# Fetching the second blocks of late operands earlier in a transformer-layer kernel on one core

## The chip, the cores and the metric

The kernel runs on one NeuronCore of a Trainium2 chip. The metric is the device time of one execution in microseconds (us). A program has five instruction queues that matter here: PE (TensorE, the matmuls), DVE (VectorE), ACT (ScalarE), POOL (GpSimd) and SP (SyncE, which here only issues DMAs). Each queue runs its instructions in the order in which they were written down, and waits at an instruction until what it depends on is done.

## The reference

The kernel computes one layer of a decoder trunk on 512 tokens (T) with a model width of 2048, a feed-forward width of 5632 and a per-layer embedding of 256. Cut to what matters:

```
h   = rmsnorm(x)
u, v_sgu, q, k, v, g_a, g_b = split(h @ w_in)
y_a = u * spatial_gating(rmsnorm(v_sgu))
y_b = stick_breaking_attention(rmsnorm(q), rmsnorm(k), v)
x  += (sigmoid(g_a) * (y_a @ w_up_a) + sigmoid(g_b) * (y_b @ w_up_b)) @ w_o
x  += (silu(gate) * up) @ w_ffn_out       # gate, up = split(rmsnorm(x) @ w_ffn_in)
x  += sigmoid(rmsnorm(x) @ w_ple_gate) * (p @ w_ple)
```

## The kernel before

**Arithmetic.** Every product is made of float32 numbers cut into a high and a low part, and so of three matmuls per product: high times high, low times high, high times low. A product of a 256-wide block of operand with weights is done either *plain* (8 products of quarter blocks) or in a *Strassen-like* form with 7 products ("S"), whose operands are sums and differences of the quarters. The weights of an S unit are summed on DVE (L373), split on ACT (high, L357) and DVE (low, L354). The operands are likewise split on ACT (L284) and DVE (L285), both called by the helper `split_into`.

**Stages, in order of time.** The combined input projection with attention and gating (0 to about 830 us); the two up projections, whose merged result is eight blocks called `mix` (to 996 us); `w_o`, which multiplies the eight `mix` blocks, giving eight output blocks j = 0 to 7 called `x1` (from 996.2 us); the small `w_ple` products; `w_ffn_in` (about 1175 to 2040 us), whose outputs are 22 blocks called `hid`; `w_ffn_out` in three passes, over 8, 8 and 6 of the `hid` blocks (starting at about 2041, 2202 and 2362 us); and the gate (about 2485 to 2661 us). `mix`, `x1`, `hid` and `x2` are stored to DRAM when they are made (SP at L1332, L1376, L1398, L1434) and fetched again as operands of the next stage.

**Late operands.** Such a fetched operand is a `Form` of kind "S" (`late_form`). It comes in two parts. The *first block* is a load of 1024 columns (512 KB) by `Form.fetch`. When the operand has its turn, a *step* splits the four quarters (ACT L284 and DVE L285, 128x1024 each) and the operand can be used plain; `HALF` says that in a stage the first four operands are used plain for the first output block (j = 0), the last four for the first two (j = 0 and 1). At that step the operand is put on a list, `seconds`. Its *second block* is the same 1024 columns again, loaded into a piece of 1280 by `Form.fetch_second`; DVE makes sums from it (L525) and three or four more tiles are split, after which the operand serves as an S operand. What is done with it depends on whether the operand's plain use is over (`form.used`) when the second block arrives: if so, a two-tile-wide sum and one split of four tiles (4x256) follow; if not, three single sums and a split of three tiles (3x256) follow at once, and a split of one tile (256) when the plain use ends.

**What sets the order.** The order of all queues is fixed when the program is built. `tick` is called once per unit of matmuls. It looks at the next three operands (`AHEAD`) of the list `builds`, fetches at most one first block, takes at most one step of the first operand in the list, and may fetch one second block. All raw blocks live in one arena, `wholes`, of 13312 columns; `fits` tries whether the pieces asked for, and 1024 more, find room there, and everything that is taken from it waits for the last user of that place. All loads and stores at the lines above stand in SP's one queue, together with the loads of the weights (L337, L339, L341).

Each operand's second load and its splits are written by the generator `plain_first`, its waiting condition by `second_arrived`. The results of `w_o` for doubled outputs (from j = 2) leave the matmul banks through `Pair.rest` (L787), and are added to the residual by `onto` (L792).

Of the kernel before, what the change touches and what calls it, by code (L numbers as in the profile page):

```python
# [39 lines left out]
AHEAD, WAIT = 3, 2  # L40
# [28 lines left out]
def hybrid_layer(  # L69
# [84 lines left out]
    parts, wholes = Arena("parts", PARTS, F32R), Arena("wholes", WHOLES, F32)  # L154
# [8 lines left out]
    def fits(sizes):  # L163

        before = parts.holes, wholes.holes
        parts.holes, wholes.holes = list(parts.holes), list(wholes.holes)
        try:
            for arena, n, how in sizes + [(wholes, 1024, "low")]:
                arena.take(n, how)
            return True  # L170
        except ValueError:
            return False
        finally:
            parts.holes, wholes.holes = before
# [15 lines left out]
    builds, seconds, stages = deque(), deque(), iter(range(1 << 30))  # L190
# [13 lines left out]
    def traced():  # L204
        return nc.cur_bb.bb.instructions

    def tick():

        clock[0] += 1
        last, units = traced()[-1], dict(newest)  # L210
        urgent = [f for f in seconds if f.used]
        sizes = []
        for f in list(builds)[: 0 if urgent else AHEAD]:
            sizes += [s for s in f.sizes if s[0] is parts]
            raw = [(wholes, 1024, "old")]
            if not f.there and f.ready() and (fits(sizes + raw) or fits(raw * 3)):
                f.fetch()
                break
        if builds and builds[0].ready() and builds[0].arrived() and fits(builds[0].sizes):
            builds.popleft().step()  # L220
        elif seconds and fits([(wholes, 5 * 256, "old")]):
            f = (urgent or seconds)[0]
            if f.used or not any(b.stage == f.stage and b.ready() and not b.there
                                 for b in list(builds)[:AHEAD]):
                f.fetch_second()
        while waiting and waiting[0][0] <= clock[0]:
            heapq.heappop(waiting)[2]()
        for i in reversed(traced()):
            if i is last:
                break  # L230
            if i.engine in units:
                tc.add_manual_dep(
                    i, units[i.engine],
                    mybir.DependencyInfo(mybir.DependencyClass.NoSync,
                                         mybir.DependencyReason.DATA),
                    reason="in its place among the units")
# [389 lines left out]
    class Pair:  # L626
# [21 lines left out]
        def add(self, kind, ws, xs, prepare=True):  # L648
# [6 lines left out]
            if kind == "P":  # L655
                for u, ((wh, wl), (xh, xl)) in enumerate(zip(ws, xs)):
                    for ps, bs in zip(self.ends(), ((3, 2), (1, 0))):
                        for k, b in enumerate(bs):
                            first = start and u + k == 0

                            mark(mm3(ps, wh[:, b], wl[:, b], xh[k], xl[k],
                                     first and not self.both, stop and u == n - 1 and k == 1,
                                     first and self.both and b < 2))
                    if prepare and u == 0:
                        prepare_late()
                    tick()
                return
# [5 lines left out]
            for i, ((name, h), (w, x)) in enumerate(zip(HALVES, PRODUCTS)):  # L673
                for u, ((wh, wl), t) in enumerate(zip(ws, xs)):
                    first, last = start and u == 0, stop and u == n - 1
                    if i < self.doubled:
                        ps = self.at(i)
                        both = ps, wh[:, w], t[:, x].rearrange("p s c -> p (s c)")
                        low = ps[:, :256], wl[:, w], t[:, x, 0]

                        work = (low, both) if u else (both, low)
                        for k, (out, l, r) in enumerate(work):
                            m = nc.tensor.matmul(out, l, r, start=first and k == 0,  # L683
                                                 stop=last and k == 1)
                        mark(m)
                    else:


                        ps = self.at(name)[:, 256 * h : 256 * h + 256]
                        ends = not (self.both and name in "yz") and (h == 1 or name == "z")  # L690
                        mark(mm3(ps, wh[:, w], wl[:, w], t[:, x, 0], t[:, x, 1],
                                 first and h == 0, last and ends))
                if stop:
                    next(mix)
                if i == 2:
                    prepare_late()
                if i in TICKS[n]:
                    tick()
# [161 lines left out]
    def ple_pair(j, weights=None):  # L860
        slot, ((wh, wl),) = weights.get() if weights else next_weights()
        if not weights:
            prepare_early()
            prepare_late()
        o = wide()
        banks = bank(), bank()
        for k in range(2):
            xh, xl = (x.own(k * T, (k + 1) * T) for x in ps_p)
            for i, ps in enumerate(banks):
                s = 2 * i + k  # L870
                mm3(ps, wh[:, s], wl[:, s], xh, xl, k == 0, k == 1)
        for i, ps in enumerate(banks):
            nc.scalar.activation(o[:, i * T : (i + 1) * T], ps, AF.Copy)
        d = tc.dram_tile([P, 1024], F32, name=nm("ple"))
        nc.sync.dma_start(out=d, in_=o)
        ple_spill[j] = d
        slots.append(slot)
        tick()
# [537 lines left out]
    for c, units in enumerate(hs):  # L1416
        first, at = at, at + len(units)
# [137 lines left out]
```

## Time and profile before

| what | us |
|---|---|
| three runs | 2667.51, 2673.16, 2673.37 |
| median of the three | 2673.16 |
| the profiled execution's own time | 2668.2 |
| its span (first to last instruction) | 2666.5 |
| PE matmul busy | 2640.4 |
| DVE busy | 2236.4 |
| ACT busy | 1413.9 |

The span is what the trace covers; the execution's own time has 1.7 us more around it. In the views, a row names the line, the engine, the operation, the tile written and the tiles read with shapes, then times in us. "idle before <- X" says how long the engine stood still ahead of that instruction and what it was waiting for. A name such as `ps` is a matmul bank, `parts` the arena of split operands, `wholes` that of raw blocks, `whi` and `wlo` the high and low parts of weights.

### The profile page before, as it was taken

To read this page: it belongs to the slowest core of one execution; us is meant where nothing else is said; L and a number is where in the kernel's file an instruction comes from. 1 tells how busy PE (TensorE), PEld (TensorE's weight loads), DVE (VectorE), ACT (ScalarE), POOL (GpSimd) and SP (SyncE) were. 2 spreads that over 40 slices of the span, in tenths; PEclk is the share of its full clock that TensorE was granted. 3 is DMA by queue.
4 is the path that set the end of the run, shared out by engine and by line. 5 is a ranking of instruction groups with operands and counts; after the bars stand their busy time and mean duration, and the time that the engine had idled before them with its cause. 6 is when DMAs were issued, how large, how long until landed. Compare 5 with 4: busy or idle time off the path is not lost.

```text
span 2666.5 us, 42598 instructions
## 1 busy us (share of the span) xinstructions
PE 2640.4 (99%) x15354; PEld 2312.4 (87%) x15354; DVE 2236.4 (84%) x3791; ACT 1413.9 (53%) x2245; POOL 453.4 (17%) x557
## 2 busy tenths in 40 slices
PE   8999999999999999999999999999999999999999
PEld 7888898888998888888888888888888888889898
DVE  8687878787887658989889888888889989989876
ACT  7656565655554334576444444444445445455643
POOL 0222322222220001101111111111110211211010
PEclk9999999999999999999999999999999999999999
DMA  7577777677775669988888878888787989988884
GB/s 227 158 190 174 185 173 187 171 182 197 179 188 186 214 212 264 239 265 223 220 218 207 210 194 207 203 203 202 197 209 223 263 220 277 226 248 246 252 229 134
DMA packets 293875, 560.16 MB, mean 210 GB/s; under 512 B 26400, under 2 KB 140832, under 8 KB 293664
## 3 DMA queue, kind: packets, MB, share of 16 engines
q1 hardware_dynamic: 231408, 442.08, 50.4%
q0 software_dynamic: 62256, 115.37, 27.0%
q8 instruction: 120, 1.97, 0.3%
q14 instruction: 91, 0.75, 0.1%
HBM read 505.97 MB, written 51.38 MB: 209 GB/s over the span
## 4 chain that ended last, share of the span: by engine, by line
PE 88%; DVE 5%; ACT 2%; DMA 2%; issue 1%; POOL 0%; SPq 0%; POOLq 0%; DVEq 0%; ACTq 0%
PE ps L683 49%; PE ps L295 10%; PE ps L296 10%; PE ps L294 10%; PE small L683 6%; DVE wlo L354 2%; DVE out L742 1%; PE small L1145 1%; PE small L1021 1%; DMA wholes<-x 1%; DMA wholes<-w_in 1%; ACT whi L357 1%; DVE wholes L373 0%; PE small L1095 0%; DVE parts L285 0%
## 5 line engine op out<-in xcount | busy, mean ns | idle before, releaser
L683 PE MATMUL ps<-parts,whi 128*128 128x512 f32 x4200 | 1404.7, 398 | 3.7 <-DVE out L787 3.1
L357 ACT ACTIVATE whi<-wholes 128x512 fp32r<-128x512 f32 (+3 forms) x941 | 872.5, 940 | 727.6 <-DVE wholes L373 270.5
L354 DVE TENSOR_TENSOR wlo<-wholes,whi 128x512 fp32r<-128x512 f32 (+3 forms) x941 | 982.7, 1079 | 65.8 <-ACT whi L357 64.0
L683 PEld LDWEIGHTS ps<-parts,wlo 128*128 128x128 f32 x4200 | 788.9, 188 | 178.4 <-DVE wlo L354 1.1
L683 PE MATMUL ps<-parts,wlo 128*128 128x256 f32 x4200 | 832.0, 279 | 0.0
L683 PEld LDWEIGHTS ps<-parts,whi 128*128 128x128 f32 x4200 | 676.4, 189 | 10.2 <-issue 4.5
L294 PE MATMUL ps<-parts,whi 128*128 128x256 f32 (+1 forms) x1822 | 598.9, 330 | 8.0 <-ACT parts L284 5.6
L295 PE MATMUL ps<-parts,whi 128*128 128x256 f32 (+1 forms) x1838 | 605.9, 330 | 0.8 <-DVE parts L285 0.8
L296 PE MATMUL ps<-parts,wlo 128*128 128x256 f32 (+1 forms) x1838 | 605.8, 330 | 0.0
L295 PEld LDWEIGHTS ps<-parts,whi 128*128 128x128 f32 x1838 | 348.4, 190 | 39.0 <-DVE parts L285 2.4
L294 PEld LDWEIGHTS ps<-parts,whi 128*128 128x128 f32 x1822 | 344.6, 190 | 41.5 <-ACT parts L284 6.7
L296 PEld LDWEIGHTS ps<-parts,wlo 128*128 128x128 f32 x1838 | 348.8, 190 | 30.8
L373 DVE TENSOR_TENSOR wholes<-wholes 128x256 f32<-128x256 f32 x822 | 345.1, 420 | 21.7 <-DMA wholes<-w_ffn_in 2.6
L742 DVE TENSOR_TENSOR out<-out,ps 128x256 f32<-128x256 f32 x490 | 202.9, 416 | 149.9 <-ACT out L739 149.4
L361 POOL DMA_DIRECT2D wholes<-w_ffn_in x170 | 148.0, 870 | 691.2 <-DVE wholes L373 197.4
L361 POOL DMA_DIRECT2D wholes<-w_in x132 | 116.3, 882 | 523.1 <-DMA wholes<-w_in 146.8
L683 PE MATMUL small<-parts,whi 128*128 128x512 f32 x480 | 190.3, 396 | 0.0
L285 DVE TENSOR_TENSOR parts<-wholes,parts 128x1024 fp32r<-128x1024 f32 (+3 forms) x148 | 138.1, 945 | 23.0 <-ACT parts L284 23.0
L284 ACT ACTIVATE parts<-wholes 128x1024 fp32r<-128x1024 f32 (+3 forms) x148 | 119.3, 830 | 55.1 <-DVE wholes L525 33.3
L739 ACT ACTIVATE out<-ps 128x256 f32<-128x256 f32 x258 | 95.7, 382 | 49.9 <-PE ps L683 46.4
L361 POOL DMA_DIRECT2D wholes<-w_ffn_out x64 | 55.6, 869 | 358.3 <-DMA wholes<-w_ffn_out 136.5
L1395 ACT ACTIVATE out<-out 128x512 f32<-128x512 f32 x44 | 27.9, 634 | 159.2 <-DVE out L1394 159.2
(123 smaller groups left out, 1750.2 us busy)
## 6 DMA issues: line engine op xcount, KB each, us to landing
wholes<-w_ffn_in SPq DMA_DIRECT2D x170, 384.0 KB, 5.6
wholes<-w_in SPq DMA_DIRECT2D x132, 384.0 KB, 5.0
wholes<-w_ffn_in SPq DMA_DIRECT2D x170, 256.0 KB, 4.8
wholes<-w_ffn_in POOLq DMA_DIRECT2D x170, 256.0 KB, 5.4
wholes<-w_in SPq DMA_DIRECT2D x132, 256.0 KB, 4.0
wholes<-w_in POOLq DMA_DIRECT2D x132, 256.0 KB, 5.0
wholes<-w_ffn_out SPq DMA_DIRECT2D x64, 384.0 KB, 6.3
wholes<-x SPq DMA_DIRECT2D x45, 512.0 KB, 5.6
```

Source lines behind the costliest of these rows:

```text
L284: return (nc.scalar.activation(hi, src, AF.Copy), nc.vector.tensor_tensor(out=lo, in0=src, in1=hi.bitcast(F32), op=ALU.subtract))
L285: nc.vector.tensor_tensor(out=lo, in0=src, in1=hi.bitcast(F32), op=ALU.subtract))
L294: nc.tensor.matmul(ps, sh, mh, start=start, stop=False)
L295: nc.tensor.matmul(ps, sh, ml, start=False, stop=False)
L296: return nc.tensor.matmul(ps, sl, mh, start=False, stop=stop)
L354: in_turn(nc.vector.tensor_tensor(out=self.lo[:, blocks], in0=r, in1=h.bitcast(F32), op=ALU.subtract))
L357: in_turn(nc.scalar.activation(h, r, AF.Copy))
L361: nc.gpsimd.dma_start(out=raw[:, 3:5], in_=self.src[:, 1:3], accum_op=ALU.add)
L373: in_turn(nc.vector.tensor_tensor(out=o, in0=x, in1=y, op=ALU.add))
L683: m = nc.tensor.matmul(out, l, r, start=first and k == 0, stop=last and k == 1)
L739: in_turn(nc.scalar.activation(out, x, AF.Copy, scale=scale))
L742: in_turn(nc.vector.tensor_tensor(out=out, in0=x, in1=y, op=op))
```

## The change

In `tick`, three things change. The fetch of a second block no longer is the alternative to an operand's step (`elif`), but may stand in the same tick. It is no longer refused while one of the next three operands of the stage has a first block that is ready and not yet fetched; instead, room must be there for the second block and for the first blocks of all of those. And the test of room comes last.

```
         if builds and builds[0].ready() and builds[0].arrived() and fits(builds[0].sizes):
             builds.popleft().step()
-        elif seconds and fits([(wholes, 5 * 256, "old")]):
+        if seconds:
             f = (urgent or seconds)[0]
-            if f.used or not any(b.stage == f.stage and b.ready() and not b.there
-                                 for b in list(builds)[:AHEAD]):
+            first = [] if f.used else [b for b in list(builds)[:AHEAD]
+                                       if b.stage == f.stage and b.ready() and not b.there]
+            if fits([(wholes, 5 * 256, "old")] + [(wholes, 1024, "old") for _ in first]):
                 f.fetch_second()
```

The changed program has one line more, so that a line from L228 on has a number higher by one (L516 is L517 there). PE, POOL and SP have as many instructions as before; DVE has 12 more and ACT 6 more, because six operands' second blocks now arrive before their plain use is over.

**Place 1: SP around the start of `w_o`.** `mix_773_8245` is the seventh of the eight `mix` blocks, `mix_774_8246` the eighth, `mix_770_8242` the fourth. SP before, from the load of the seventh operand's first block on:

```order
L516 DMA wholes_74<-mix_773_8245 128x1024
L339 DMA wholes_74<-w_o 128x2x256
L341 DMA wholes_74<-w_o 128x768
L1332 DMA mix_774_8246<-wholes_74 128x1024
L337 DMA wholes_74<-w_o 128x1024
L516 DMA wholes_74<-mix_774_8246 128x1024
L337 DMA wholes_74<-w_o 128x1024
L516 DMA wholes_74<-mix_770_8242 128x1024
L516 DMA wholes_74<-xT 128x1024
```

SP of the change, from the last load of `xT` ahead of the same store on:

```order
L517 DMA wholes_74<-xT 128x1024
L340 DMA wholes_74<-w_o 128x2x256
L342 DMA wholes_74<-w_o 128x768
L1333 DMA mix_774_8246<-wholes_74 128x1024
L338 DMA wholes_74<-w_o 128x1024
L517 DMA wholes_74<-mix_773_8245 128x1024
L517 DMA wholes_74<-mix_774_8246 128x1024
L338 DMA wholes_74<-w_o 128x1024
L517 DMA wholes_74<-mix_771_8243 128x1024
L517 DMA wholes_74<-mix_773_8245 128x1024
```

The seventh operand's first block moved from two weight loads ahead of the store of the eighth block to behind it, next to the eighth operand's first block; its place in the arena overlaps what that store reads, so that it waits for the store to land. ACT and DVE split the eighth operand first and then the seventh. The fourth operand's second block is not in the rows of the change because it went far ahead, to directly behind that operand's first block.

**Place 2: DVE ahead of the first doubled output of `w_o` (j = 2).** L787 (L788 in the change) takes the results out of the banks that j = 2 is to reuse. DVE before:

```order
L525 TENSOR_TENSOR wholes_74<-wholes_74 128x256
L285 TENSOR_TENSOR parts_73<-wholes_74,parts_73 128x256
L525 TENSOR_TENSOR wholes_74<-wholes_74 128x256
L285 TENSOR_TENSOR parts_73<-wholes_74,parts_73 128x256
L354 TENSOR_TENSOR wlo0_77<-wholes_74,whi0_76 128x1280
L354 TENSOR_TENSOR wlo0_77<-wholes_74,whi0_76 128x512
L285 TENSOR_TENSOR parts_73<-wholes_74,parts_73 128x3x256
L787 TENSOR_TENSOR out_1049_9527<-ps_1044_9512,out_1049_9527 128x512
L787 TENSOR_TENSOR out_1049_9527<-ps_1043_9505,out_1049_9527 128x512
```

DVE of the change, up to the same two rows and the two behind them:

```order
L286 TENSOR_TENSOR parts_73<-wholes_74,parts_73 128x256
L374 TENSOR_TENSOR wholes_74<-wholes_74 128x256
L286 TENSOR_TENSOR parts_73<-wholes_74,parts_73 128x256
L374 TENSOR_TENSOR wholes_74<-wholes_74 128x256
L788 TENSOR_TENSOR out_1042_9541<-ps_1037_9521,out_1042_9541 128x512
L788 TENSOR_TENSOR out_1042_9541<-ps_1036_9514,out_1042_9541 128x512
L793 TENSOR_TENSOR wholes_74<-wholes_74,out_1042_9541 128x1024
L355 TENSOR_TENSOR wlo0_77<-wholes_74,whi0_76 128x1280
L355 TENSOR_TENSOR wlo0_77<-wholes_74,whi0_76 128x512
```

The low split of a weight slot (two rows) and a split of three operand tiles stood directly ahead of L787; in the change that weight split stands behind, and the sums and the three-tile splits of the late second blocks are some ten rows further ahead.

**Place 3: SP around the start of the first pass of `w_ffn_out`.** In the program of before `hid_1200` is the first operand of the pass, `hid_1206` the seventh, `hid_1207` the eighth; in the change the same blocks are `hid_1199`, `hid_1205` and `hid_1206`. SP before:

```order
L516 DMA wholes_74<-hid_1206_10919 128x1024
L516 DMA wholes_74<-hid_1207_10920 128x1024
L339 DMA wholes_74<-w_ffn_out 128x2x256
L341 DMA wholes_74<-w_ffn_out 128x768
L337 DMA wholes_74<-w_ffn_out 128x1024
L516 DMA wholes_74<-hid_1200_10913 128x1024
L516 DMA wholes_74<-hid_1201_10914 128x1024
```

SP of the change at the same place:

```order
L517 DMA wholes_74<-hid_1199_10920 128x1024
L517 DMA wholes_74<-hid_1205_10926 128x1024
L340 DMA wholes_74<-w_ffn_out 128x2x256
L342 DMA wholes_74<-w_ffn_out 128x768
L338 DMA wholes_74<-w_ffn_out 128x1024
L517 DMA wholes_74<-hid_1206_10927 128x1024
L517 DMA wholes_74<-hid_1200_10921 128x1024
```

The first operand's second block took the place of the seventh operand's first block, which moved one place back, and the eighth operand's first block moved behind three weight loads, where the first operand's second block had been.

## The prediction

> **What bounds the kernel now.** I read the page first, for the engine that is never idle.
>
> ```profile
> span 2666.5 us, 42598 instructions
> PE 2640.4 (99%) x15354; PEld 2312.4 (87%) x15354; DVE 2236.4 (84%) x3791; ACT 1413.9 (53%) x2245; POOL 453.4 (17%) x557
> PE 88%; DVE 5%; ACT 2%; DMA 2%; issue 1%; POOL 0%; SPq 0%; POOLq 0%; DVEq 0%; ACTq 0%
> ```
>
> PE is busy for 99% of the span and holds 88% of the chain that ended last. The change has as many matmuls as before, so it can win only PE's idle time, and what the clock loses behind it. The change acts where late operands exist, from about 830 us on. So I read PE's waits in that stretch next.
>
> ```profile
> PE ps L683 <- DVE out L787: 3.1, 1, 3.1
> PE small L932 <- DVE diag L930: 1.0, 1, 1.0
> PE ps L295 <- DVE parts L285: 0.8, 2, 0.5
> PE ps L294 <- ACT out L873: 0.6, 1, 0.6
> PE ps L294 <- ACT parts L284: 0.4, 2, 0.2
> ```
>
> These five rows (us in total, times, longest) sum to 5.9 us. The 1.0 at L932 belongs to a norm that the change leaves alone; 3.1 is one wait for L787 (place 2), and 1.8 are five small ones at stage starts. The next view gives the stretch of the big wait, with busy time per engine and the granted clock (PEclk, the column behind POOL).
>
> ```profile
> 1039.00:1044.20 5.20, 5.20 (x30) 4.26 (x28) 5.20 (x12) 3.02 (x5) 0.40 (x1) 1.00 0.98 239
> 1044.20:1047.30 3.10, 0.08 (x1) 0.00 (x0) 3.10 (x5) 0.70 (x3) 0.89 (x1) 1.00 0.90 327
> 1047.30:1048.60 1.30, 1.23 (x7) 1.15 (x8) 1.30 (x3) 0.00 (x0) 0.00 (x0) 1.00 0.87 153
> 1048.60:1052.00 3.40, 3.40 (x14) 2.92 (x13) 3.10 (x5) 2.70 (x3) 0.88 (x1) 0.51 1.01 278
> ```
>
> The wait costs twice. Behind it the clock is 0.51 for 3.40 us, which by the clock loses 3.40 x 0.49 = 1.67 us; by the count, 14 matmuls at 5.20/30 = 0.173 us are 2.43 us of work, a loss of 0.97. As some matmul records can be missing, I take **1.4**, with 0.97 and 1.67 as ends.
>
> **The stall at 1044 us.** DVE is full there (5.20 of 5.20, 3.10 of 3.10), so L787 waits for its turn. Its timeline (start, duration):
>
> ```profile
> 1043.00 0.42 DVE L525 TENSOR_TENSOR wholes<-wholes 128x256 f32<-128x256 f32 x1
> 1043.33 0.42 DVE L285 TENSOR_TENSOR parts<-wholes,parts 128x256 fp32r<-128x256 f32 x1
> 1043.67 2.09 DVE L354 TENSOR_TENSOR wlo<-wholes,whi 128x1280 fp32r<-128x1280 f32 x2
> 1045.67 0.95 DVE L285 TENSOR_TENSOR parts<-wholes,parts 128x768 fp32r<-128x768 f32 x1
> 1046.54 1.28 DVE L787 TENSOR_TENSOR out<-ps,out 128x512 f32<-128x512 f32 x2
> ```
> ```profile
> 1047.37 0.47 PE L683 MATMUL ps<-parts,whi 128*128 128x512 f32 x1 [3.09 <-DVE out L787]
> ```
>
> PE needed the bank at 1047.37 - 3.09 = 1044.28. Place 2 shows that the change puts the weight split behind L787 and the three-tile split far ahead: 1046.54 - 1043.67 = 2.87 us go from directly ahead of it. Four sums (L525), 0.34 us each by the starts of these rows, go too: 1.36. L787 would start at 1046.54 - 2.87 - 1.36 = 1042.3 and end at 1043.6, with 0.7 us to spare. The moved rows run before, where the late operands' loads come earlier. So the stall goes whole: -3.1 and -1.4, **-4.5** (ends -4.06 and -4.76; zero if DVE's earlier rows are late). Next late is the weight split now behind L787, whose weights are for a later unit.
>
> **The new late operand (place 1).** The price is in the seventh `mix` operand's first block. SP's issues before, the landing time of such loads around `w_o`, and what the splits take:
>
> ```profile
> 992.98 0.33 SPq L516 DMA_DIRECT2D wholes<-mix  x1
> ...
> 998.41 0.33 SPq L1332 DMA_DIRECT2D mix<-wholes  x1
> 999.55 0.33 SPq L337 DMA_DIRECT2D wholes<-w_o  x1
> 1001.83 0.33 SPq L516 DMA_DIRECT2D wholes<-mix  x1
> ```
> ```profile
> wholes<-mix SPq DMA_DIRECT2D x7, 512.0 KB, 6.0
> ```
> ```profile
> L357 ACT ACTIVATE whi<-wholes 128x1280 fp32r<-128x1280 f32 x405 | 514.7, 1271 | 302.1 <-PE ps L683 129.0 <-PE ps L295 53.7 <-issue 51.3
> L285 DVE TENSOR_TENSOR parts<-wholes,parts 128x1024 fp32r<-128x1024 f32 x72 | 86.9, 1220 | 15.9 <-ACT parts L284 15.9
> L284 ACT ACTIVATE parts<-wholes 128x1024 fp32r<-128x1024 f32 x72 | 74.5, 1051 | 30.4 <-DVE wholes L525 10.7 <-DMA wholes<-y 10.0 <-DMA wholes<-mix 8.3
> L284 ACT ACTIVATE parts<-wholes 128x256 fp32r<-128x256 f32 x36 | 13.2, 401 | 0.0
> L525 DVE TENSOR_TENSOR wholes<-wholes 128x512 f32<-128x512 f32 x13 | 8.7, 685 | 0.1
> ```
>
> The seventh block was issued at 992.98 and the eighth at 1001.83, when the store of 998.41 had landed (1001.83 - 998.41 = 3.4). In the change both go at 1001.83 and about 1002.2; at 6.0 to land the later is there at 1008.2. ACT splits the eighth first (1.05: 1009.2), then both halves of a weight slot (1.79, the row at 1007.09 below: 1011.0), two 256 splits (0.40 each, overlapping a little, 0.7: 1011.7) and the seventh (1.05: 1012.75). DVE ends its part of the eighth at 1010.4, then the weight slot (2.09, as at 1043.67: 1012.6), four short rows (1.35: 1013.95) and the seventh's low part (1.22: **1015.2**).
>
> ```profile
> 1007.09 1.79 ACT L357 ACTIVATE whi<-wholes 128x1280 fp32r<-128x1280 f32 x2 [2.77 <-PE ps L295]
> 996.20:1012.56 16.36, 16.36 (x73) 13.52 (x73) 12.05 (x16) 7.68 (x10) 0.87 (x1) 1.00 0.93 288
> 1012.56 0.39 PE L294 MATMUL ps<-parts,whi 128*128 128x512 f32 x1
> ```
>
> At j = 0 each plain operand takes 12 matmuls, and six of them fill 996.20 to 1012.56; the matmul at 1012.56 is the first on the seventh operand, the next, 0.23 us on, needs its low part. PE would wait from 1012.8 to 1015.2, 2.4 us, less a few matmuls of the next output that the order puts between. Earlier landings give about 0.6, ones 1.3 us later 3.1. I take **+2.2**. Whether that trips the clock is bounded by two other stretches:
>
> ```profile
> 21.22:24.64 3.42, 1.63 (x8) 0.91 (x6) 3.25 (x7) 3.09 (x5) 0.00 (x0) 1.00 0.84 274
> 24.64:28.05 3.41, 3.41 (x10) 2.56 (x9) 3.41 (x7) 2.35 (x4) 0.00 (x0) 0.50 0.97 346
> ```
> ```profile
> 2505.50:2508.90 3.40, 2.42 (x13) 1.53 (x12) 2.18 (x7) 2.17 (x4) 0.00 (x0) 1.00 1.00 332
> ```
>
> Idle 1.79 of 3.42 us was followed by half clock; idle 0.98 of 3.40 stays at 1.00. The 2.2 us come in two pieces, which may lie in one such window or in two: I take half of 1.4, **+0.7** (ends 0 and 1.67).
>
> The Trainium skill, page "TensorE: Matmul & The Clock Gate", section "What's actually happening", puts half rate after at least one idle window of about 3.4 us. By it neither the 3.09 nor the new 2.2 us would cool the clock, and the sum below would be -3.1 + 2.2 - 0.6 = -1.5; but the two rows with 0.51 and 0.50 behind waits of 3.09 and 1.79 us say otherwise, and the measurement decides.
>
> **The other stage starts.** The first pass of `w_ffn_out`:
>
> ```profile
> 2034.90 2.60 SPq L516 DMA_DIRECT2D wholes<-hid  x2
> ...
> 2046.77 2.06 SPq L516 DMA_DIRECT2D wholes<-hid  x2
> ```
> ```profile
> wholes<-hid SPq DMA_DIRECT2D x8, 512.0 KB, 5.8
> ```
>
> The eighth operand's first block goes from the second load of the pair at 2034.90 to 2046.77 (place 3): 9.6 us later. It lands at 2052.6 and, with both splits and what stands ahead of them, is ready at 2055 to 2057. The pass starts at about 2041 with plain operands of 16.36/6 = 2.73 us, so its eighth is used from 2060.1. Some 3 to 5 us of cover: **0**, and if that cover is gone, up to +3 and a cold window. In the other passes and at the gate, loads move by one or two places, and second blocks come a few us earlier; of the five small waits (1.8 us) I take a third away: **-0.6** (ends 0 and -1.8).
>
> The added instructions (12 DVE, 6 ACT): six operands have one 3x256 and one 256 split (0.95 + 0.42) for one 4x256 (1.22), and two more sums of 0.42 for one of 0.68, about 0.3 us of DVE each, 1.9 in all. At 84% DVE has the room; two of them fall ahead of place 2, inside the 0.7 us to spare. **0** (up to +0.6).
>
> **The sum:** -4.5 + 2.2 + 0.7 - 0.6 = -2.2 us, against the profiled execution's 2668.2: 2666.0. The median is 5.0 us above that execution; against 2673.16 the forecast is **2671.0**. The ends: -4.76 - 1.8 = -6.6 with no new cost; -4.06 + 3.1 + 1.67 + 3 + 1.67 = +5.4.
>
> **The rivals.**
>
> *No new late operand (0.18).* The blocks land 2 us sooner or PE's order fills the gap: -4.5 - 0.6 = -5.1, 2668.1. For it: the medians hide landings of 1 to 2 us less. Against: ACT and DVE still put the eighth operand and a weight slot first.
>
> *What the median has above the profiled execution is of this kind too (0.14).* Two of three runs lie 5.0 us above it; if those are such stalls, the change removes them as well: -5.1 - 5.0 = -10.1, 2663.1, faster by over 0.3%. No trace shows such a run.
>
> *The late seventh block decides: slower (0.18).* The chain of waits has one load of the same size that took far longer:
>
> ```profile
> 1183.07 10.31 DMA wholes<-x
> ```
>
> If the pair at 1001.83, beside two weight loads, lands like that, in 10.3 us and not 6.0, the seventh operand is 2.2 + 4.3 = 6.5 us late, with two cold windows (+3.3). From about 1 us of extra delay on, DVE's rows ahead of L787 slip past its 0.7 to spare, and the gain at 1044 is given back; the first pass, 4.3 us later too, is just covered. Net +6.5 + 3.3 - 0.6 = +9.2, 2682.4.
>
> *Nothing moves (0.06).* The loads change places, but all is hidden under PE's 99%: 2673.2. Against it, place 2 visibly reorders what PE waits for.
>
> *The skill's clock rule (0.02):* no cold windows at all, -1.5, 2671.7; the page is named above.
>
> **How the numbers follow.** The forecast has 0.42. About 0.3%, 8 us, is what a measurement of this kernel can tell from no change. Faster by more is the second rival, 0.14; slower by more the third, 0.18; all else, 0.42 + 0.18 + 0.06 + 0.02 = 0.68, lies within. The range takes the ends of the sum from the outer runs: 2667.51 - 6.6 = 2661 and 2673.37 + 5.4 = 2679; it holds the forecast, the first two rivals and the small ones, and leaves out the slower one.
>
> **What would show it.** Right: no wait of PE for L788 near 1044, no 0.5 clock behind it; a new wait of PE for operand splits (L285, L286) at 1012 to 1015 us of 0.6 to 3.1 us; no wait at 2055 to 2061. The term of -4.5 is wrong if PE still waits there; +2.2 is wrong if no idle time stands at 1012. The whole is wrong if PE's idle time appears in a stage that I left at zero, the `w_ple` products or the gate above all, where I compared orders and no times.

## The result, and the profile after

The change makes the kernel slower: 2678.11 us median against 2669.97 us for the kernel before, each over eight runs. These medians are 8.1 us apart; the ratio worked out from all sixteen runs is 1.0024 (95% interval 1.0014 to 1.0033), some 6.4 us. Repeated beside the last experiments it gave 1.0027 (1.0017 to 1.0037). I had forecast 2.2 us faster.

The page of the changed kernel's profiled execution (2676.37 us, span 2674.7) has the same lines at its head:

```profile
span 2674.7 us, 42607 instructions
...
PE 2642.6 (99%) x15354; PEld 2313.5 (86%) x15354; DVE 2233.0 (83%) x3803; ACT 1414.4 (53%) x2251; POOL 457.1 (17%) x557
...
PE 88%; DVE 6%; ACT 2%; DMA 2%; issue 2%; POOL 1%; SPq 0%; DVEq 0%; POOLq 0%; ACTq 0%
```

They tell almost nothing: PE has 99% in both. PE's waits from 830 us on (line numbers from L228 on are higher by one) tell more:

```profile
PE ps L295 <- ACT parts L285: 4.6, 1, 4.6
PE ps L296 <- DVE parts L286: 2.1, 3, 0.9
PE ps L295 <- ACT out L874: 1.9, 1, 1.9
PE ps L297 <- DVE wlo L355: 0.6, 1, 0.6
PE small L933 <- DVE diag L931: 0.4, 1, 0.4
```

The 3.1 us wait for L787 is gone, and a wait of 4.6 us for an operand split and one of 1.9 us for ACT's copy of a `w_ple` product (L874) are there instead. The first is at the place I had named. PE's timeline there:

```profile
1012.16 0.39 PE L297 MATMUL ps<-parts,wlo 128*128 128x512 f32 x1
1017.14 1.43 PE L295 MATMUL ps<-parts,whi 128*128 128x512 f32 x3 [4.59 <-ACT parts L285]
...
1019.66 0.80 PE L296 MATMUL ps<-parts,whi 128*128 128x512 f32 x1 [0.66 <-DVE parts L286]
```

The reader sees the high part of the seventh `mix` operand come 4.59 us late, and its low part another 0.66. Then the stretch behind it, in pieces of 3.4 us (the column behind POOL is the granted clock):

```profile
1012.60:1016.00 3.40, 0.00 (x0) 0.00 (x0) 2.12 (x2) 3.21 (x5) 0.00 (x0) 0.89 0.28 113
1016.00:1019.40 3.40, 1.86 (x5) 1.37 (x5) 3.40 (x7) 2.88 (x4) 0.00 (x0) 0.50 0.78 228
1019.40:1022.80 3.40, 3.14 (x7) 2.51 (x8) 3.37 (x7) 0.00 (x0) 0.43 (x1) 0.50 0.85 290
1022.80:1026.20 3.40, 3.40 (x11) 2.69 (x10) 0.28 (x1) 0.85 (x1) 0.45 (x1) 0.60 0.98 320
1026.20:1029.60 3.40, 3.40 (x25) 3.14 (x24) 3.12 (x4) 2.05 (x2) 0.89 (x1) 1.00 0.70 118
```

The clock is half through almost three pieces, though PE works without a gap from 1019.66 us on. Taken as one stretch, half clock lasts 10.24 us, 7.69 of them with PE at work:

```profile
1015.25:1025.49 10.24, 7.69 (x19) 6.00 (x20) 7.79 (x13) 4.47 (x7) 0.88 (x1) 0.50 0.80 257
```

To see where time goes, I number PE's matmuls and subtract the start of the matmul with the same number in the trace of before (discarded matmuls of an experiment are left out). A lag of PE is thus a sum of all that has happened up to that place; where a few matmuls changed places, it is off by some tenths. Both sides are single executions, and that of before (2668.2 us) is some 3 us under the medians of before beside the experiments (2670.9 to 2671.6), so the last column shows a loss too large by about that much.

| lag of PE behind before, us, at | 994 | 1021 | 1055 | 1170 | 1204 | 1273 | 2049 | end |
|---|---|---|---|---|---|---|---|---|
| the change | -0.2 | 9.2 | 4.3 | 4.3 | 7.6 | 7.8 | 7.8 | 8.2 |
| same tick alone | -0.5 | -0.5 | -1.5 | -1.2 | -0.1 | 0.6 | 0.6 | 3.3 |
| relaxed condition alone | 0.9 | 9.5 | 4.6 | 4.7 | 6.7 | 12.0 | 11.9 | 14.1 |
| room kept for blocks not ready | 0.2 | 0.2 | -4.3 | -4.3 | -3.2 | -0.7 | -0.7 | 4.0 |
| the change in `w_o` only | 0.5 | 9.2 | 4.3 | 4.4 | 5.5 | 10.1 | 10.0 | 12.3 |
| room kept, in `w_o` only | 0.0 | 0.0 | -4.4 | -4.4 | -4.1 | -2.7 | -2.7 | 0.7 |
| the change in x1 only | 0.1 | 0.1 | 3.3 | 3.3 | 9.9 | 9.8 | 9.8 | 13.6 |
| room kept in `w_o`, x1 high | 3.5 | 3.5 | -0.6 | -0.6 | -0.4 | 1.0 | 1.0 | 2.4 |

For the change: 9.3 us are lost at the seventh operand (from 0.2 ahead to 9.2 behind); 4.9 come back by 1055 us; 3.3 are lost between 1170 and 1204 us, at the wait at 1179; 0.6 in all the rest. That leads to the 8.2 us between the two spans.

### The profile page after: what moved, and what is told of

Same layout as the page of the kernel before. It is cut to its first block, busy times and chain, and to the rows that moved or that the text cites. A ratio compares the mean times of both kernels' runs of the same rounds, so it can differ in the third digit from the quotient of the medians.

```text
span 2674.7 us, 42607 instructions
## 1 busy us (share of the span) xinstructions
PE 2642.6 (99%) x15354; PEld 2313.5 (86%) x15354; DVE 2233.0 (83%) x3803; ACT 1414.4 (53%) x2251; POOL 457.1 (17%) x557
## 4 chain that ended last, share of the span: by engine, by line
PE 88%; DVE 6%; ACT 2%; DMA 2%; issue 2%; POOL 1%; SPq 0%; DVEq 0%; POOLq 0%; ACTq 0%
PE ps L684 49%; PE ps L296 10%; PE ps L297 10%; PE ps L295 10%; PE small L684 6%; DVE wlo L355 2%; DVE out L743 1%; DMA wholes<-w_in 1%; PE small L1146 1%; ACT whi L358 1%; PE small L1022 1%; DVE wholes L374 0%; PE small L1096 0%; PE small L1203 0%; DVE parts L286 0%
```

## The experiments

All ratios are to the kernel before, run beside each kernel, with 95% intervals. The medians of before were 2671.13 us beside the first four, 2670.91 beside the next four and 2671.63 beside the last four.

| run | median us | ratio | interval |
|---|---|---|---|
| same tick alone | 2670.42 | 0.9998 | 0.9989 to 1.0007 |
| relaxed condition alone | 2681.44 | 1.0042 | 1.0029 to 1.0055 |
| room kept for blocks not ready | 2672.21 | 1.0007 | 0.9998 to 1.0016 |
| the change, 20 matmuls more | 2677.18 | 1.0024 | 1.0014 to 1.0034 |
| the change in `w_o` only | 2683.18 | 1.0049 | 1.0036 to 1.0061 |
| room kept, in `w_o` only | 2670.83 | 1.0001 | 0.9993 to 1.0010 |
| the change in x1 only | 2682.57 | 1.0043 | 1.0030 to 1.0055 |
| the change, 34 matmuls more | 2677.76 | 1.0028 | 1.0017 to 1.0039 |
| room kept in `w_o`, x1 high | 2667.37 | 0.9983 | 0.9974 to 0.9993 |
| same tick in `w_o`, x1 held and low | 2669.55 | 0.9990 | 0.9981 to 1.0000 |
| before, 20 matmuls more | 2670.59 | 0.9993 | 0.9984 to 1.0002 |
| the change again | 2678.43 | 1.0027 | 1.0017 to 1.0037 |

**The two halves.** Same tick alone, against before:

```
-        elif seconds and fits([(wholes, 5 * 256, "old")]):
+        if seconds and fits([(wholes, 5 * 256, "old")]):
```

> The first half of the change alone: a second block may be fetched in the same tick as an operand's step, but is still held back while first blocks of the stage are pending. Theory A (the loss of the change is the seventh mix operand's late first block, 4.6 us of wait and some 3.6 us of half clock at 1012 to 1025 us, and about 4 us around 1179 us; both come from the other half): here the seventh operand's first block is ahead of the store again, no wait at 1012, and the weight split is no longer ahead of L787, so the 3.1 us wait at 1044 goes: 4 to 5 us below before, ratio about 0.998. Theory B (the extra loads in one tick crowd the one queue of loads, and many small waits add up): slower than before by 3 us or more, with waits spread over the stage starts.

Of theory A only the first half came: there is no wait at 1012 us. The ratio is 0.9998: not slower, as theory B had it, but the gain at 1044 us is all but missing too (the lag goes from -0.5 to -1.5). The row of PE's waits for L787, the first of its two waits, and DVE's timeline:

```profile
PE ps L683 <- DVE out L787: 3.4, 2, 2.4
```
```profile
1043.80 0.50 PE L683 MATMUL ps<-parts,whi 128*128 128x512 f32 x1 [2.38 <-DVE out L787]
```
```profile
1034.62 1.10 DVE L525 TENSOR_TENSOR wholes<-wholes 128x256 f32<-128x256 f32 x3 [3.50 <-DMA wholes<-mix]
...
1043.06 0.68 DVE L787 TENSOR_TENSOR out<-ps,out 128x512 f32<-128x512 f32 x1
...
1045.66 0.68 DVE L787 TENSOR_TENSOR out<-ps,out 128x512 f32<-128x512 f32 x1
```

The weight split is no longer directly ahead of the first L787, and that row runs 3.5 us earlier than in before (1043.06 for 1046.54). But PE's order has moved along, and PE asks for this bank earlier too, at 1043.80 - 2.38 = 1041.42 us and not at 1044.28. DVE stood idle for 3.50 us until the last second block of `w_o` had landed, which is more than either wait. In before it stood idle there as well, for 1.94 us:

```profile
1035.10 1.10 DVE L525 TENSOR_TENSOR wholes<-wholes 128x256 f32<-128x256 f32 x3 [1.94 <-DMA wholes<-mix]
```

So the two rows ahead of L787 were not all that held it up; the landing counts as well.

The other half alone, the condition of the change behind the old `elif`:

```
-        if seconds:
+        elif seconds:
             f = (urgent or seconds)[0]
             first = ...
```

> The second half alone: fetch of a second block remains the alternative to a step, but is no longer held back by pending first blocks as long as they would have room. Theory A: nearly the whole time of the changed kernel, ratio 1.002 to 1.003, with the wait of about 4.6 us at 1012 us, half clock behind it, and no wait at 1044. Theory B: about the time of before, within 2 us.

As theory A said, and worse: 1.0042. The lags at 1021 and 1055 us (9.5 and 4.6) are those of the change. The loss in `w_o` belongs to the relaxed condition. A further 5.3 us are lost between 1204 and 1273 us, where PE waits 2.5 us for the low part of a weight slot.

**Room for blocks that are not ready yet.** The change, with one word less:

```
-                                       if b.stage == f.stage and b.ready() and not b.there]
+                                       if b.stage == f.stage and not b.there]
```

> The change, but room must also be there for first blocks among the next three operands that are not yet ready to be fetched. In its order the seventh mix operand's first block stands ahead of the store of the eighth again, and the fourth operand's second block directly behind that store, ahead of the eighth's first block. Theory A: no wait at 1012 us, none at 1044: 3 to 5 us below before, ratio about 0.9985, unless the eighth operand, which now lands one load later, is late at 1015.3 us (then up to 2 us are lost again). Theory B: as slow as the changed kernel, since as many second blocks are fetched early.

In `w_o` theory A holds in full: PE has no wait from 990 to 1060 us and is 4.3 us ahead at 1055. DVE runs the same rows ahead of L788 (L787 before) as in the run of same tick alone, but without the idle time:

```profile
1040.23 0.68 DVE L788 TENSOR_TENSOR out<-ps,out 128x512 f32<-128x512 f32 x1
...
1042.83 0.68 DVE L788 TENSOR_TENSOR out<-ps,out 128x512 f32<-128x512 f32 x1
```

Each stands 2.8 us earlier than there. So the gain at 1044 us exists. But the total does not show it (1.0007): in the one trace 3.6 us are lost again between 1170 and 1273 us, and 4.7 from 2049 us on (the table of lags).

**The half clock.** The change, with discarded matmuls ahead of the first one on the seventh operand (20, later 34):

```
+            if forms is ms_list[0] and j == 0 and k == 6:
+                warm = small_bank()
+                x = forms[0].plain()[0][0]
+                for _ in range(20):
+                    m = nc.tensor.matmul(warm, x[:, 0, :P], x, start=True, stop=True)
+                mark(m)
             p.add(...)
```

> The changed kernel with 20 matmuls of 512 columns more, whose result is thrown away, on PE just ahead of the first matmul on the seventh mix operand. At 0.227 us each they take 4.5 us, about the 4.59 us that PE waits there, and keep it busy. Theory A, with the loss behind the wait put down to the clock: the wait shrinks to under 1 us, the granted clock stays at 1.0 from 1012 to 1025 us, and the kernel is 3 to 4 us faster than the changed one, ratio to before 1.000 to 1.001. If the 3.6 us behind the wait have another cause (late operands behind the seventh), the time stays that of the changed kernel or rises, ratio 1.0024 or more.

A miss: 1.0024, as slow as the change. The blocks landed a little later in this execution, so that waits of 1.07 and 1.69 us remained behind the 20 matmuls, and these were enough for the clock:

```profile
1017.40:1020.80 3.40, 1.50 (x5) 1.05 (x6) 3.40 (x9) 1.95 (x3) 0.00 (x0) 1.00 0.73 232
1020.80:1024.20 3.40, 3.40 (x9) 2.62 (x8) 3.09 (x5) 0.84 (x1) 0.87 (x1) 0.51 1.00 348
```

Half clock for one piece of 3.4 us here, where the change had almost three. With 34:

> The changed kernel with 34 matmuls of 512 columns whose result is thrown away (20 left 2.8 us of the wait open) ahead of the first matmul on the seventh mix operand: 7.7 us at 0.227 each, to about 1019.7 us, when that operand's low part was ready. Clock theory: PE never idles over 1 us there, the granted clock stays 1.0, and PE is 6.5 to 7.5 us behind before at 1021 us against 9.2 for the changed kernel; the time is about 2 us under the changed kernel's, ratio 1.0015 to 1.002. If what follows the wait is slow for another reason, the lag at 1021 us stays 9 us or more.

```profile
1012.68:1016.00 3.32, 3.32 (x16) 2.77 (x15) 1.75 (x2) 2.84 (x4) 0.00 (x0) 1.00 0.55 218
1016.00:1020.40 4.40, 4.40 (x22) 3.62 (x21) 4.40 (x9) 2.64 (x4) 0.00 (x0) 1.00 0.73 207
1020.40:1023.80 3.40, 3.40 (x17) 2.81 (x16) 3.40 (x6) 1.37 (x2) 0.88 (x1) 1.00 0.96 338
```

PE has no gap, the clock stays at 1.00, and the lag at 1021 us is 7.8 us against 9.2, a little over the expected 6.5 to 7.5: DVE ended the seventh operand's low part at 1019.3 us, and the discarded matmuls ran to 1020.4. So the half clock stands for at least 1.3 us of the 9.2, as far as two executions can tell. From the trace of the change, 7.69 us of work at half clock are a loss of 3.8 us, and the two waits are 5.25. In the total this drowns: 1.0028, where 2 us less than the change had been expected. The clock is a part of the loss, and not the larger one.

**Stage by stage.** The change in force for one stage only, the rule of before for all others. Stage 1 is `w_o`; the run of x1 has a 2 in its place:

```
+            if f.stage in (1,):
+                room = [(wholes, 1024, "old") for _ in first]
+                if fits([(wholes, 5 * 256, "old")] + room):
+                    f.fetch_second()
+            elif not stepped and fits([(wholes, 5 * 256, "old")]):
+                if not [b for b in first if b.ready()]:
+                    f.fetch_second()
```

> The change in force for the operands of w_o only; all other stages keep the rule of before. Theory A (two places carry the result: at w_o the late seventh operand costs about 9 us by 1035 us and the absent wait at 1044 gives 4.5 to 4.9 back; at the w_ple products another 3.4 us are lost): PE is 4 to 5 us behind before at 1055 us and stays there, ratio 1.0015 to 1.002. Theory B (the loss is a property of fetching second blocks early anywhere): clearly less than half of the changed kernel's loss, ratio under 1.001.

> The change in force for the operands of w_ffn_in (x1) only; all other stages keep the rule of before, so that the wait at 1044 us stays. The first x1 operand's second block goes ahead of the last one's first block. Theory A: PE is level with before at 1170 us and about 3.4 us behind at 1205 us, with a wait of about 2 us for ACT's copy of a w_ple product (L874 of the changed kernel) and half clock behind it; ratio 1.001 to 1.0015. Theory B: the wait at 1179 us in the changed kernel came from what w_o had shifted, and is absent here: ratio 1.000.

Neither run came out as expected. With the change in `w_o` only, theory A holds up to 1170 us: PE is 4.3 us late at 1055. But it is 12.3 late at the end (1.0049); 4.6 us of that are lost between 1204 and 1273 us, where PE waits 1.9 us for operand splits and the clock is half from 1215.1 to 1218.5; which block brought this was not followed. With the change in x1 only, PE should have been level at 1170 us and was 3.3 us behind (below). The wait at 1179 us is absent, as theory B had it, so that wait came with what `w_o` had shifted; but the ratio is 1.0043 and not 1.000, since 4.46 us are lost at 1202 us for another late block:

```profile
1206.69 1.22 PE L303 MATMUL ps<-parts,whi 128*128 128x512 f32 x2 [4.46 <-ACT parts L293]
```

In its order the last x1 operand's first block had moved behind three more weight loads, and ACT's work on it began when it landed, at 1203.1 us. A stage's rule also moves blocks in stages whose rule is unchanged (the next run has two such blocks): all share the one arena, and where a hole is decides when a first block can go. This run shows one more thing. Its SP and DVE orders around L787 (L796 here) are those of before, and yet:

```profile
PE ps L692 <- DVE out L796: 5.1, 1, 5.1
```
```profile
1037.14 1.10 DVE L534 TENSOR_TENSOR wholes<-wholes 128x256 f32<-128x256 f32 x3 [4.10 <-DMA wholes<-mix]
```

The same order waited 3.1 us in one execution and 5.1 in another, because the second block landed 2 us later (DVE's row is at 1037.14 us and not at 1035.10).

The room kept in `w_o` only (the code above, `first` without `b.ready()`):

> In w_o only, second blocks may be fetched in the same tick and ahead of pending first blocks, but with room kept also for those of the next three operands that are not ready yet; all other stages keep the rule of before. Theory A: as in the run that kept such room everywhere, no wait of PE from 996 to 1060 us, 4.3 us ahead of before at 1055 us; the later stages as before: 2667 us, ratio 0.9984. Theory B: the gain at 1044 is lost again in the later stages by other arrangements of the arena, ratio 1.000 or more.

At 1055 us theory A is right to a tenth (-4.4). In the total theory B is (1.0001): 1.7 us are lost by 1273 us, 3.4 after 2049 us. In the order, the sixth `hid` operand's first block no longer goes early in `w_ffn_in` but with the last ones, and the eighth's goes behind three weight loads. That these two blocks carry the loss is argued from the order.

**An arrangement that keeps the first blocks where they were.** As the last run, and the second blocks of x1 at the high end of the arena; or the same tick in `w_o`, x1's second blocks held until all first blocks are fetched, and at the low end:

```
-            lambda size=1024: load(spill[n, j], size), ...
+            lambda size=1024: load(spill[n, j], size,
+                                   "high" if n == "x1" and size > 1024 else "old"), ...
```

> As the run with kept room in w_o only, but the second blocks of the x1 operands are put at the high end of the arena. In its order the later stages' first blocks then stand where they stand in before (the sixth hid operand's first block is fetched early again, the eighth's ahead of three weight loads), and the seventh mix operand's is early too. Theory now (what decides is whether a first block stands later than in before; the absent wait at 1044 us is worth 4.4 us): the 4.4 us gained at w_o stay to the end but for about 1 us, 2667 us, ratio 0.9985, end 3 to 5 us ahead of before in the profile. Rival (later stages lose again whatever the order, because second blocks as such crowd ACT and DVE): the gain is gone by 2480 us, ratio 1.000.

> Same tick allowed in w_o, the x1 operands' second blocks held until all their first blocks are fetched and put at the low end of the arena, all else as before. By the order it has fewest first blocks later than in before, and of the mix operands only the sixth's second block is earlier. Theory: w_o as in the run of the same-tick half alone, since the last second block of w_o is issued where it was (a wait at 1041 to 1046 us of 2 to 3.5 us remains), later stages as before: 2669 to 2671 us, ratio 0.999 to 1.000. Rival (fewest late first blocks is all that counts): ratio 0.998.

By their times both came as the theory had them. The first is faster than both kernels: 0.9983 (0.9974 to 0.9993), 4.3 us between the medians. From 990 to 1060 us PE waits once:

```profile
PE ps L693 <- DVE out L797: 0.6, 1, 0.6
```

PE gains 4.1 us between 994 and 1055. The one trace does not bear out the rest: I had expected it 3 to 5 us ahead of before at the end, and it is 2.4 behind. This execution was the slowest of the eleven and was 3.5 us behind at 994 us already, ahead of the stages that its edits reach; but it also loses 3 us again behind 1055 us, where I had expected 1. The time over many runs is the better judge of the whole; that the gain is kept because the later first blocks stand where they stood is not shown by the trace. The second gives 0.9990 (0.9981 to 1.0000) with two waits left at L797, 2.6 us together.

**Who sets the wait at 1044 us.** The kernel before, with the 20 discarded matmuls:

> The kernel before with 20 matmuls of 512 columns more, whose result is thrown away, ahead of the first matmul on the seventh mix operand: 4.5 us more work of PE at 1012 us. Theory (L787 comes late because the last second block of w_o lands late and DVE is full behind it, whatever PE does): the wait of 3.1 us at 1044 and the half clock behind it (1.4) vanish, and the added 4.5 us cost nothing by 1055 us: ratio 1.000. Rival (loads and DVE wait for PE to free buffers, so that the wait moves along with PE): 4.5 us slower, ratio 1.0017, with the wait still there.

By the times the theory holds: 0.9993 (0.9984 to 1.0002), so 4.5 us of added PE work cost nothing that can be measured, and the rival's 1.0017 is excluded. The one trace speaks for the rival's mechanism: a wait of 2.2 us is left, and PE is 3.6 us behind at 1055, not 0.

```profile
PE ps L683 <- DVE out L787: 2.2, 1, 2.2
```
```profile
1038.74 1.10 DVE L525 TENSOR_TENSOR wholes<-wholes 128x256 f32<-128x256 f32 x3 [1.55 <-DMA wholes<-mix]
```

DVE gets the seventh operand's second block 3.6 us later than in before (1038.74 for 1035.10), and L787 runs 3.6 us later (1050.18). The chain can be followed back to PE: that load waits for the store of the first x1 block to land, SP issued this store at 1027.82 us and not at 1023.80, and the store waits for the DVE row that adds PE's results of the first output. So here most of the added time was passed on to the wait. The order is not quite that of before either: that store went one weight load earlier, and the last two second blocks changed places. As the same order gave 3.1 and 5.1 us above, one trace can't settle how much of the 4.5 the wait takes up in an average execution; it stays open.

**The change again.**

> The changed kernel again, beside these runs on one chip: ratio 1.002 to 1.003; in its profile a wait of 4 to 5.5 us at 1012 us and one of 1.5 to 2.5 us at 1179 us, no wait at 1044.

1.0027, with waits at 1012 and 1179 us and none at 1044. The second is in its range, the first 0.1 us over (row of the waits: longest 5.6).

```profile
PE ps L295 <- ACT parts L285: 5.9, 2, 5.6
...
PE ps L295 <- ACT out L874: 2.1, 1, 2.1
```

## Why the prediction was wrong

**The step that failed is the new late operand, "+2.2" and "+0.7".** The mechanism was right, and the place to a few tenths of a us; the size was not: the waits were 5.25 us and the half clock cost some 4. I timed the pair of loads by SP's issue of before, 1001.83, and 6.0 us of landing. SP's and ACT's rows of the change:

```profile
1000.22 0.33 SPq L1333 DMA_DIRECT2D mix<-wholes  x1
1001.35 0.33 SPq L338 DMA_DIRECT2D wholes<-w_o  x1
1005.26 0.85 SPq L517 DMA_DIRECT2D wholes<-mix  x2
```
```profile
wholes<-mix SPq DMA_DIRECT2D x3, 512.0 KB, 7.1
...
mix<-wholes SPq DMA_DIRECT2D x1, 512.0 KB, 5.0
```
```profile
1012.79 1.06 ACT L285 ACTIVATE parts<-wholes 128x1024 fp32r<-128x1024 f32 x1 [7.50 <-DMA wholes<-mix]
```

The store that the seventh block waits for went 1.8 us later than in before (1000.22 for 998.41), took 5.0 us to land and not 3.4, and the loads 7.1 and not 6.0: 1.8 + 1.6 + 1.1 = 4.5 us, which is why ACT started at 1012.79 and not at 1008.2. From there the chain of splits took 4.35 us to PE's start at 1017.14; I had 4.55. So a chain of a store and the loads behind it was summed at the times of one execution in which the seventh block did not stand in that chain. It was also an early one. In the eight kernels whose seventh block goes ahead of the store, the traces have the store issued between 998.4 (before, the earliest) and 1003.1 us and landed in 2.6 to 4.5 us, so the 1.8 us need not come from the change. In the six kernels or repeats with the late block it was issued at 1000.2 to 1002.6 us, landed in 4.1 to 5.7, and the second load of the pair landed at 1012.8 to 1014.2 us; none came near the 1008.2 that I had put. The waits were 4.59 + 0.66 = 5.25 us, and with them the clock was half for 10.24 us and not for half a piece: 9.3 us in all, for 2.9 forecast.

My slower rival, with loads of 10.3 us, had put 9.8 there and +9.2 in all. It came near the 8.2 us between the spans in part by luck: the loads took 7.1 us, the gain at 1044 us was not given back as it said, and the loss at 1179 us is not in it.

**The stall at 1044 us, -4.5: the size right (-4.9), but not for the reason given.** I had L788 at 1042.3 us. It ran later than in before:

```profile
1049.74 1.28 DVE L788 TENSOR_TENSOR out<-ps,out 128x512 f32<-128x512 f32 x2
```

PE, 9.2 us behind, needed the bank only at 1044.28 + 9.15 = 1053.4, and L788 ended at 1051.0. Had the two rows that the change moved (2.87 us) still stood directly ahead, it would have ended at 1053.9 at the latest, by an estimate from these rows: at most 0.5 us too late for PE, and not 3.1. So most of the wait went because PE came late, and the move of the rows was worth the rest and a margin; no run separates the two. The size is thus luck in part, and in `w_o` the change leaves PE 4.3 us behind. Undoing the late seventh block and keeping early second blocks gave the gain that I had argued, for the reason that I had argued: 4.5 and 4.4 us, with L788 at 1040.2 and 1042.8.

**The small waits, -0.6.** They became +3.3 at 1179 us. PE waits there for a bank that ACT empties at L874, behind a square, a split and gains of x1 blocks:

```profile
1178.52 1.06 ACT L945 ACTIVATE out<-wholes 128x1024 f32<-128x1024 f32 x1
1179.46 1.05 ACT L285 ACTIVATE parts<-wholes 128x1024 fp32r<-128x1024 f32 x1
1180.41 1.08 ACT L874 ACTIVATE out<-ps 128x512 f32<-128x512 f32 x2
```
```profile
1181.06 0.50 PE L295 MATMUL ps<-parts,whi 128*128 128x512 f32 x1 [1.91 <-ACT out L874]
```

Behind the 1.91 us the clock was half again (0.66 and 0.50 in the two pieces of 3.4 us from 1181.4 on). All runs in which `w_o` had its late seventh block have this wait (1.9 to 2.5 us), and in their orders the first x1 operand's second block stands seven weight loads further ahead than in before; those without it have 0.6 to 1.1. PE's lateness alone does not bring the wait: in the run of x1 only, PE was 3.3 us late there and the wait was 0.6; that block stood four weight loads further ahead. That the earlier block fills ACT is argued from the timeline; no run moves it alone.

**The first pass of `w_ffn_out`, 0:** right. The eighth operand's block went behind three weight loads, and no wait stands there (lag 7.8 before it, 7.4 behind).

**The added instructions, 0:** nothing in the runs speaks against it.

## What to carry to other kernels

A rule that hands out places in a shared buffer is a scheduler: look first at which load it moves later, not at which it moves earlier, and do so in every stage behind it. When a load has to wait for a store to leave its place, its chain is store issue, store landing and load landing, each at the worst duration of that stretch and not at the median of another. And a wait that vanishes behind a new wait is no gain; count the two as one.

## What the runs showed of the hardware

Half clock needs no idle stretch of 3.4 us: 1.9 us idle of 3.40 (1017.40 to 1020.80, with the 20 matmuls) brought 0.51 for the next 3.4 us, as 1.79 had in before. Here the Trainium skill, "TensorE: Matmul & The Clock Gate", section "What's actually happening", asks for one idle window of about 3.4 us before half rate; the rows above show less to be enough.

But such an amount of idle time does not always do it. In the run of same tick alone PE was idle for 2.38 us of 3.40, and the clock stayed full:

```profile
1041.00:1044.40 3.40, 1.02 (x7) 0.66 (x6) 3.40 (x7) 3.10 (x5) 0.00 (x0) 1.00 0.97 254
1044.40:1047.80 3.40, 2.38 (x15) 1.86 (x14) 3.40 (x6) 0.29 (x1) 0.89 (x1) 1.00 0.93 342
```

What divides the two cases no run here shows. Once lost, the clock came back late: in the change PE worked without a gap from 1019.66 us, and the clock was half until 1025.49. The half stretches at the places discussed here last 3.41, 6.83 or 10.24 us, once, twice or three times the same length.

Transfers of 512 KB vary from execution to execution: the store of the eighth `mix` block landed in 2.6 to 5.7 us over the fourteen traces, and the two loads behind it in 5.5 to 7.1 us over the six with the late block.
